# Both maps' attention scores in one PSUM tile of two banks, and PSUM pools opened anew for each stage

## Chip, core and metric

The kernel runs on one core of a Trainium2 chip. The metric is device time in microseconds (us), the median of several runs. The engines are TensorE (PE; PEld is its weight load), VectorE (DVE), ScalarE (ACT), GpSimd (POOL) and SyncE (SP), which issues the loads.

## What is computed

One layer of an encoder over 512 positions of width 1024: a normed and modulated input is projected, three mixers (differential attention, two gated recurrences) run on it, their results are projected up, gated and summed, and an MLP follows. The part that the change touches is the differential attention, with 4 heads, two maps of 64 dimensions in each, and blocks of 128 queries:

```python
scores = jnp.einsum('bhiqd,bhikd->bhiqk', qb, k).astype(jnp.float32) * scale
scores = scores - slopes[:, None, None, None] * dist
p = jax.nn.softmax(scores, axis=-1)
w = p[:, :, 0] - lam * p[:, :, 1]
return jnp.einsum('bhqk,bhkv->bhqv', w.astype(v.dtype), v)
```

Index i is the map: two softmaxes over the same 512 keys, of which the second is subtracted with a weight.

## The kernel before

All large products are made of fp32r matmuls in three parts: a weight and an input are each split into a high and a low part, and `mm3` (lines 219 to 222) issues high by high, high by low and low by high into one PSUM bank. One such matmul streams 512 columns through all 128 rows of the array.

**PSUM.** It has 8 banks of 128x512 fp32. Pool `pm` has 3 for projections (`ps_mm`), `pl` has 3 (`ps_lv`) and `pt` 2 (`ps_ms`). `pl` serves the scans' level scores first and the attention's scores later; `pt` serves transposes, the attention's output and the norms' statistics. The pools are open from the first stages to the kernel's end.

**Attention** (`attention(hd)`, lines 784 to 818). For each of 4 heads and each of 4 blocks of queries, two tiles of `pl` are taken, one for each map. Each map has three matmuls (q high by k high, q high by k low, q low by k high), 6 in all, 96 in the kernel. A map has 64 dimensions, so map 0 uses rows 0 to 63 of the array and map 1 rows 64 to 127 (line 795). Then DVE adds the distance penalty and takes the row maximum (line 800, one operation for each map, which is the only reader of the score's bank), ACT takes the exponential (line 803), DVE normalises and subtracts the maps (lines 806 to 809), PE transposes the result in four pieces (line 812, tile `wt`) and ACT copies these out (line 814). After the four blocks of a head PE multiplies with the values (line 817, tile `oa`), and `head_norm` (lines 630 to 639) norms the head: a square on ACT, a matmul with a matrix of constants for the mean (line 634, tile `An..ms`), a logarithm and an exponential on ACT, a product on DVE, and a split into a high part (ACT, `An..oh`) and a low part (DVE, `An..ol`).

**Work around it.** `merge_bc(m)` for m = 0 to 7 projects the gates `gb`, `gc` (24 matmuls each) and the two recurrences' results `up` (6 matmuls each), combines them on DVE (lines 834 and 836, tiles `gbs`, `gcs`, `part`), and then takes four tiles of the modulation's weights, `ada`: each is loaded (512 KB) and reduced by one DVE operation (line 164). `att_proj` projects q and k of heads 2 and 3, `proj_a` the gates `ga`. `pump(NA)` in `attention` starts pieces of this work between the steps of a block. Behind the attention, a loop over m (lines 860 to 874) multiplies the four normed heads with `wup_a` into a bank of `pm` (`upa`), after `ga` of the same m.

**Order.** In this stage the order on each engine is not the order of the code: the framework's scheduler places each instruction where its own timeline lets it start, and each engine then runs its list in that order. A tile's pool hands out its buffers in turn, and the first writer of a buffer waits for the last reader of what it held. Raw weights and `ada` tiles share one ring of four SBUF buffers (tag `wr` of pool `wp`), and all their loads stand in SyncE's queue in order, each waiting for its buffer to come free. `weights` (lines 209 to 217) loads a raw tile, and ACT and DVE make its high part (line 215) and its low part (line 216).

Of the kernel before, what the change touches and what calls it, by code (L numbers as in the profile page):

```python
# [11 lines left out]
F32 = mybir.dt.float32  # L12
# [5 lines left out]
PSUM = bass.MemoryType.PSUM  # L18

P = 128  # L20
S = 512
# [33 lines left out]
def tile_trunk(ctx, tc, xT, cols, lam_p, w2blk, ada, slab, wtok, wlr, wck, wcq, wg, watt, wgate, wup_bc, wup_a, wout,  # L55
# [4 lines left out]
    def pool_of(name, n, side="left"):  # L60
        return tc.tile_pool(name=name, bufs=n, side=side, reuse_waits="tile")
# [15 lines left out]
    sm = ms_.enter_context(pool_of("sm", 4))  # L77
    sm.tile([P, 8], F32, tag="fill", name="smfill")
    pm = ctx.enter_context(tc.tile_pool(name="pm", bufs=3, space=PSUM))
    pl = ctx.enter_context(tc.tile_pool(name="pl", bufs=3, space=PSUM))  # L80

    def st(name, dt=F32, pool=None):
        return (pool or gp).tile([P, S], dt, tag="t", name=name)
# [4 lines left out]
    def ps_lv(name):  # L88
        return pl.tile([P, S], F32, tag="lv", name=name)

    def ps_ms(name):
        return pt.tile([P, S], F32, tag="ms", name=name)
# [102 lines left out]
    def pump(n):  # L195

        while queue and n > 0:
            try:
                next(queue[0])
                n -= 1  # L200
            except StopIteration:
                queue.popleft()
# [67 lines left out]
    with tc.tile_pool(name="ad0", bufs=8, side="right", reuse_waits="tile") as ad0, \  # L270
# [54 lines left out]
        for k in range(KT):  # L325
# [12 lines left out]
            f = t  # L338
# [13 lines left out]
                for u in us:  # L352
                    mm3(slab_ps[u], wh[:, u * P:(u + 1) * P], wl[:, u * P:(u + 1) * P], hi, lo, False, k == KT - 1)
        lb, neglam, gsub, gb40, masks, bm, w2b, nd = small_operands()
    pt = ctx.enter_context(tc.tile_pool(name="pt", bufs=2, space=PSUM))

    def proj(src, name):
        wh, wl = weights(src, name, [P, KT, P])
# [271 lines left out]
    def head_norm(o, n, blk, g, extra, pool, dst):  # L630
        sq = st(n + "sq", pool=pool)
        A.activation(sq, o, AF.Square)
        ms = ps_ms(n + "ms")
        T.matmul(ms, blk, sq, start=True, stop=True)
        rs = rstd_of(ms, n + "rs", pool)
        V.scalar_tensor_tensor(sq, o, g, rs, ALU.mult, ALU.mult)  # L636
        if extra is not None:
            V.scalar_tensor_tensor(sq, sq, 0.5, extra, ALU.mult, ALU.mult)
        return split(sq, n + "o", dst)
# [133 lines left out]
    zs.close()  # L773
    ys.close()
    zs, ys = ExitStack(), ExitStack()
    oap = zs.enter_context(pool_of("oap", 8))
    fp = ys.enter_context(pool_of("fp", 8, "right"))
    es = ExitStack()
# [5 lines left out]
    def attention(hd):  # L784
        slope = 2.0 ** (-2 * (hd + 1))
        qh, ql, kh, kl = qk[hd]
        wT = [st(f"wT{hd}{k}", pool=wtp) for k in range(4)]
        for qt in range(4):
            qs = slice(qt * P, (qt + 1) * P)
            e = []  # L790
            mx = sm.tile([P, 8], F32, tag="mx", name=f"mx{hd}{qt}")
            sc = [ps_lv(f"s{hd}{qt}{i}") for i in range(2)]
            for n_, (q_, k_) in enumerate(((qh, kh), (qh, kl), (ql, kh))):
                for i in range(2):
                    rr = slice(64 * i, 64 * i + 64)
                    T.matmul(sc[i], q_[rr, qs], k_[rr, :], start=n_ == 0, stop=n_ == 2)  # L796
            pump(NA)
            for i in range(2):
                s_ = st(f"e{hd}{qt}{i}", pool=ep)
                V.tensor_tensor_reduce(s_, sc[i], nd[:, 384 - P * qt:896 - P * qt], scale=slope, scalar=-3e38,  # L800
                                       op0=ALU.add, op1=ALU.max, accum_out=mx[:, i:i + 1])
                V.tensor_scalar(mx[:, 2 + i:3 + i], mx[:, i:i + 1], -1.0, None, ALU.mult)  # L802
                A.activation(s_, s_, AF.Exp, bias=mx[:, 2 + i:3 + i], accum_out=mx[:, 4 + i:5 + i])  # L803
                e.append(s_)
            pump(NA)
            V.reciprocal(mx[:, 6:8], mx[:, 4:6])
            V.tensor_tensor(mx[:, 7:8], mx[:, 7:8], neglam, ALU.mult)
            V.tensor_scalar(e[0], e[0], mx[:, 6:7], None, ALU.mult)  # L808
            V.scalar_tensor_tensor(e[0], e[1], mx[:, 7:8], e[0], ALU.mult, ALU.add)  # L809
            ps = ps_ms(f"wt{hd}{qt}")  # L810
            for k in range(4):
                T.transpose(ps[:, k * P:(k + 1) * P], e[0][:, k * P:(k + 1) * P], ident)  # L812
            for k in range(4):
                A.copy(wT[k][:, qs], ps[:, k * P:(k + 1) * P])  # L814
        o = ps_ms(f"oa{hd}")
        for k in range(4):
            T.matmul(o, av[k][:, hd * P:(hd + 1) * P], wT[k], start=k == 0, stop=k == 3)  # L817
        oa.append(head_norm(o, f"An{hd}", ones128, gsub, None, ep, oap))
# [35 lines left out]
    for hd in range(4):  # L854
        need(f_att[hd])
        attention(hd)
# [19 lines left out]
    zs.close()  # L876
    ys.close()
    ms_.close()

    gtm = lambda m: modc[:, 16 + m:17 + m]  # L880
    amlp = const.tile([P, 8], F32, name="amlp")
# [304 lines left out]
    with tc.manual_schedule(engines=ENGINES):  # L1186
# [227 lines left out]
        for u in range(4, 16):  # L1414
            g, i = divmod(u, 4)
# [161 lines left out]
```

## Time and profile before

| | us |
|---|---|
| median of 3 runs (lowest, highest) | 866.3 (865.47, 867.59) |
| time of the profiled execution | 868.18 |
| its span | 866.3 |
| PE busy | 848.4 (98%) |
| PE's weight loads busy | 718.4 (83%) |
| DVE busy | 602.9 (70%) |
| ACT busy | 431.3 (50%) |
| chain of work that ended last, on PE | 94% |

The span runs from the first to the last instruction of the execution. An engine's busy time counts its operations alone; matmuls are pipelined, so that the distance between two starts, not the length of one, is what a matmul costs. A timeline gives the start, the length, the engine, the line of the code and the tiles; a number in brackets is idle time before the instruction, with what ended it. `x2` stands for two instructions shown in one row.

### The profile page before, as it was taken

Reading aid. Unit: us, or ns where it says so; the run is one execution under the profiler, and the core shown is the slowest. Engines: PE = TensorE matmul, PEld = TensorE weight load, DVE = VectorE, ACT = ScalarE, POOL = GpSimd, SP = SyncE. Lnnn points to the kernel's source line nnn. Section 1 sums busy time; section 2 is a strip of 40 time slices with the busy share of each in tenths; the row PEclk is TensorE's granted clock in tenths of the full one; section 3 lists DMA queues with packets and bytes.
Section 4 is the critical chain, followed back from the end, with each engine's and each line's share of the span. In section 5 each row is a group of like instructions: output and inputs, shape, how many; then the busy total and the mean of one; then the engine's idle time right before and its main releaser. Section 6 shows DMA issues by size and latency. Waiting matters only on the chain.

```text
span 866.3 us, 14040 instructions
## 1 busy us (share of the span) xinstructions
PE 848.4 (98%) x5632; PEld 718.4 (83%) x5632; DVE 602.9 (70%) x1077; ACT 431.3 (50%) x783; POOL 25.1 (3%) x33
## 2 busy tenths in 40 slices
PE   6999999999999999999999999999999999999995
PEld 3797888888777776777788899999999999999885
DVE  7968899595677685866166658766666666766445
ACT  5577887554354454446344436833444443444323
POOL 3700000000000000000000000000000000000000
PEclk9999999999999999999999999999999999999998
DMA  9933111112636454553134501332323323333202
GB/s 342 400 109 121 51 50 51 50 42 70 207 110 206 135 162 144 206 193 122 61 98 145 175 21 55 115 100 98 98 98 98 98 98 104 113 104 119 76 23 98
DMA packets 32817, 103.15 MB, mean 119 GB/s; under 512 B 3665, under 2 KB 6129, under 8 KB 32753
## 3 DMA queue, kind: packets, MB, share of 16 engines
q1 hardware_dynamic: 32752, 102.26, 35.9%
q8 instruction: 44, 0.72, 0.3%
q14 instruction: 21, 0.16, 0.1%
HBM read 100.15 MB, written 2.10 MB: 118 GB/s over the span
## 4 chain that ended last, share of the span: by engine, by line
PE 94%; DVE 3%; ACT 1%; DMA 1%; issue 0%; SPq 0%; DVEq 0%; ACTq 0%
PE w L222 7%; PE w L221 7%; PE w L220 7%; PE s L796 2%; PE ou L221 2%; PE ou L222 2%; PE ou L220 2%; PE tp L375 2%; PE oa L817 2%; PE tp L376 2%; PE tp L377 2%; PE sl L221 1%; PE sl L222 1%; PE sl L220 1%; PE up L220 1%; PE wt L812 1%
## 5 line engine op out<-in xcount | busy, mean ns | idle before, releaser
L164 DVE CUSTOM_DVE_ANT_0 ada<-ada,cb,col 128x1024 f32<-128x1024 f32 x32 | 41.1, 1283 | 32.9 <-DMA ada<-ada 32.9
L1157 DVE SCALAR_TENSOR_TENSOR x<-w,modc,x 128x512 f32<-128x512 f32 (+1 forms) x35 | 24.6, 703 | 32.6 <-PE w L222 32.6
L803 ACT ACTIVATE e<-e,mx 128x512 f32<-128x512 f32 x32 | 22.9, 719 | 23.9 <-DVE mx L802 23.9
L800 DVE CUSTOM_DVE_ANT_0 e<-s,nd 128x512 f32<-128x512 f32 x32 | 20.8, 685 | 0.0
L164 DVE CUSTOM_DVE_ANT_0 ada<-ada,cps,col 128x1024 f32<-128x1024 f32 x16 | 19.9, 1271 | 0.9 <-ACT cb L295 0.9
L814 ACT COPY wT<-wt 128x128 f32<-128x128 f32 x64 | 12.2, 279 | 13.4 <-PE wt L812 13.3
L1120 DVE SCALAR_TENSOR_TENSOR r<-r 128x512 f32<-128x512 f32 x24 | 16.5, 688 | 0.4
L817 PE MATMUL oa<-wT,av 128*128 128x512 f32 x32 | 14.4, 592 | 0.0
L915 DVE SCALAR_TENSOR_TENSOR x<-ou,modc,x 128x256 f32<-128x256 f32 (+1 forms) x12 | 6.8, 570 | 10.6 <-PE ou L222 10.6
L809 DVE SCALAR_TENSOR_TENSOR e<-e,mx,e 128x512 f32<-128x512 f32 x16 | 12.0, 750 | 0.3
L869 DVE SCALAR_TENSOR_TENSOR gas<-gas,upa 128x512 f32<-128x512 f32 x8 | 5.4, 686 | 9.0 <-PE upa L222 9.0
L336 ACT ACTIVATE hf<-hf,modc,amix 128x512 f32<-128x512 f32 x7 | 5.7, 817 | 12.0 <-DVE modc L164 8.3
L926 ACT ACTIVATE q<-x 128x256 f32<-128x256 f32 (+1 forms) x11 | 5.2, 470 | 13.0 <-DVE x L915 13.0
L1166 ACT ACTIVATE q<-x 128x256 f32<-128x256 f32 (+1 forms) x9 | 4.6, 514 | 13.4 <-DVE x L1157 13.4
L817 PEld LDWEIGHTS oa<-wT,av 128*128 128x128 f32 x32 | 6.0, 189 | 6.1 <-issue 5.5
L812 PEld LDWEIGHTS wt<-ident,e 128*128 128x128 f32 x64 | 7.6, 140 | 3.0 <-issue 0.7
L812 PE MATMUL wt<-ident,e 128*128 128x128 f32 x64 | 9.8, 275 | 0.0
L309 POOL TENSOR_TENSOR hf<-x,rx 128x512 f32<-128x512 f32 x7 | 9.5, 1357 | 0.0
L872 ACT ACTIVATE mgh<-part 128x512 fp32r<-128x512 f32 x8 | 5.0, 632 | 7.2 <-DVE part L870 7.2
L636 DVE SCALAR_TENSOR_TENSOR Hn1sq<-H1o,col,Hn1rsl 128x512 f32<-128x512 f32 x1 | 0.8, 750 | 10.9 <-ACT Hn1rsl L178 10.9
L636 DVE SCALAR_TENSOR_TENSOR An3sq<-oa,gsub,An3rsl 128x512 f32<-128x512 f32 x1 | 0.8, 751 | 10.8 <-ACT An3rsl L178 10.8
L808 DVE TENSOR_SCALAR e<-e,mx 128x512 f32<-128x512 f32 x16 | 7.7, 481 | 0.0
(7148 smaller groups left out, 3318.2 us busy)
## 6 DMA issues: line engine op xcount, KB each, us to landing
ada<-ada SPq DMA_DIRECT2D x48, 512.0 KB, 4.4
x<-xT SPq DMA_DIRECT2D x16, 256.0 KB, 4.4
outT<-o SPq DMA_DIRECT2D x8, 256.0 KB, 2.2
w10r<-w SPq DMA_DIRECT2D x2, 512.0 KB, 6.5
w11r<-w SPq DMA_DIRECT2D x2, 512.0 KB, 5.2
w12r<-w SPq DMA_DIRECT2D x2, 512.0 KB, 3.7
w13r<-w SPq DMA_DIRECT2D x2, 512.0 KB, 3.6
w14r<-w SPq DMA_DIRECT2D x2, 512.0 KB, 3.2
```

Of the source, the lines that this page charges most:

```text
L164: V.tensor_tensor_reduce(w, w, c_, scale=1.0, scalar=C("ada_b", ADA_BLK[u]), op0=ALU.mult, op1=ALU.add, accum_out=o)
L220: T.matmul(ps, wh, xh, start=first, stop=False)
L221: T.matmul(ps, wh, xl, start=False, stop=False)
L222: T.matmul(ps, wl, xh, start=False, stop=last)
L375: T.matmul(o, hh, wh, start=k == 0, stop=False)
L376: T.matmul(o, hh, wl, start=False, stop=False)
L377: T.matmul(o, hl, wh, start=False, stop=k == KT - 1)
L800: V.tensor_tensor_reduce(s_, sc[i], nd[:, 384 - P * qt:896 - P * qt], scale=slope, scalar=-3e38, op0=ALU.add, op1=ALU.max, accum_out=mx[:, ...
L803: A.activation(s_, s_, AF.Exp, bias=mx[:, 2 + i:3 + i], accum_out=mx[:, 4 + i:5 + i])
L812: T.transpose(ps[:, k * P:(k + 1) * P], e[0][:, k * P:(k + 1) * P], ident)
L817: T.matmul(o, av[k][:, hd * P:(hd + 1) * P], wT[k], start=k == 0, stop=k == 3)
L1157: V.scalar_tensor_tensor(x, self.ps[:, sl], modc[:, 40 + self.m:41 + self.m], x, ALU.mult, ALU.add)
```

## The change

The PSUM pools `pl` and `pt` move to an own stack, `banks`, which is closed and opened again ahead of the attention and behind it. For the attention there is a pool `pd` with one buffer of two banks, which holds the scores of both maps of one block, and `pt` has three banks where it had two; `pm` keeps its three. Behind the attention `pl` and `pt` have three and two banks again.

```diff
-    pl = ctx.enter_context(tc.tile_pool(name="pl", bufs=3, space=PSUM))
+    banks = ctx.enter_context(ExitStack())
+    pl = banks.enter_context(tc.tile_pool(name="pl", bufs=3, space=PSUM))
...
-    pt = ctx.enter_context(tc.tile_pool(name="pt", bufs=2, space=PSUM))
+    pt = banks.enter_context(tc.tile_pool(name="pt", bufs=2, space=PSUM))
...
     zs, ys = ExitStack(), ExitStack()
+    banks.close()
+    pd = banks.enter_context(tc.tile_pool(name="pd", bufs=1, space=PSUM))
+    pt = banks.enter_context(tc.tile_pool(name="pt2", bufs=3, space=PSUM))
...
-            sc = [ps_lv(f"s{hd}{qt}{i}") for i in range(2)]
+            both = pd.tile([P, 2, S], F32, tag="s", name=f"s{hd}{qt}")
+            sc = [both[:, i, :] for i in range(2)]
...
     ms_.close()
+    banks.close()
+    pl = banks.enter_context(tc.tile_pool(name="pl2", bufs=3, space=PSUM))
+    pt = banks.enter_context(tc.tile_pool(name="pt3", bufs=2, space=PSUM))
```

No operation is added or taken away. Line numbers of the changed kernel are higher by 7 at the scores (796 becomes 803) and by 1 in `mm3` (220 to 222 become 221 to 223). The scheduler orders the stage anew. Three places show it. The digits behind `s`, `e` and `mx` are head and block, then the map; a number behind an underscore is the buffer's.

**PE, scores of head 0.** Before, the three matmuls of map 1 of block 1 (`s011`) stand alone, those of map 0 some rows earlier; block 2 follows six rows later:

```order
L222 MATMUL up02_2836<-Gn1oh_2685,ubc0l_2721 128x512
L796 MATMUL s011_2801<-k0h_2383,qh0_2284 128x512
L796 MATMUL s011_2801<-k0l_2384,qh0_2284 128x512
L796 MATMUL s011_2801<-k0h_2383,ql0_2285 128x512
L220 MATMUL up10_2864<-Hn0oh_1402,ubc1h_2860 128x512
L221 MATMUL up10_2864<-Hn0ol_1403,ubc1h_2860 128x512
L222 MATMUL up10_2864<-Hn0oh_1402,ubc1l_2861 128x512
L220 MATMUL up10_2864<-Hn1oh_1740,ubc1h_2860 128x512
L221 MATMUL up10_2864<-Hn1ol_1741,ubc1h_2860 128x512
L222 MATMUL up10_2864<-Hn1oh_1740,ubc1l_2861 128x512
L796 MATMUL s020_2893<-k0h_2383,qh0_2284 128x512
L796 MATMUL s021_2894<-k0h_2383,qh0_2284 128x512
```

In the changed kernel (`x2` is one matmul of each map) the six of block 1 stand together:

```order
L223 MATMUL up12_2878<-Gn1oh_2685,ubc1l_2867 128x512
L803 MATMUL s01_2807<-k0h_2383,qh0_2284 128x512 x2
L803 MATMUL s01_2807<-k0l_2384,qh0_2284 128x512 x2
L803 MATMUL s01_2807<-k0h_2383,ql0_2285 128x512 x2
L221 MATMUL aq2p_2927<-h0h_254,aq2h_2923 128x512
L222 MATMUL aq2p_2927<-h0l_255,aq2h_2923 128x512
```

What moved: all 16 blocks now have their six score matmuls in one piece, where the order before had 18 pieces: 13 with three matmuls of one map or six of two, one of three that four transposes cut in two, and four of nine matmuls, in which the second map of one block is followed by the next block (or a whole block by the first map of the next).

**DVE, head 2, block 0.** Before, the two operations that read the scores (`e200`, `e201`) stand behind three `ada` tiles:

```order
L164 ISA ada37_3767,modc_158<-ada37_3767,cb_157,col_129 128x1024
L164 ISA modc_158 128x1
L216 TENSOR_TENSOR gb5l_3625<-gb5r_3622,gb5h_3624 128x1024
L164 ISA ada38_3770,modc_158<-ada38_3770,cb_157,col_129 128x1024
L164 ISA modc_158 128x1
L882 SCALAR_TENSOR_TENSOR amlp_4638<-modc_158,col_129 128x8
L800 ISA e200_3507,mx20_3469<-s200_3470,nd_555 128x512
L800 ISA mx20_3469 128x1
L800 ISA e201_3511,mx20_3469<-s201_3471,nd_555 128x512
L800 ISA mx20_3469 128x1
L800 ISA e210_3591,mx21_3555<-s210_3556,nd_555 128x512
```

In the changed kernel they stand behind four of the next group of `ada` tiles, which follow `gcs4`, `ubc5l` and `part4` directly:

```order
L165 ISA ada40_3941,modc_158<-ada40_3941,cb_157,col_129 128x1024
L165 ISA modc_158 128x1
L165 ISA ada41_3944,modc_158<-ada41_3944,cb_157,col_129 128x1024
L165 ISA modc_158 128x1
L217 TENSOR_TENSOR gb6l_3775<-gb6r_3772,gb6h_3774 128x1024
L165 ISA ada42_3947,modc_158<-ada42_3947,cb_157,col_129 128x1024
L165 ISA modc_158 128x1
L165 ISA ada43_3950,modc_158<-ada43_3950,cb_157,col_129 128x1024
L165 ISA modc_158 128x1
L807 ISA e200_3506,mx20_3469<-s20_3470,nd_555 128x512
L807 ISA mx20_3469 128x1
L807 ISA e201_3510,mx20_3469<-s20_3470,nd_555 128x512
```

What moved: the readers of block 0 of head 2 went behind `ada40` to `ada43`. On PE the next block's scores (`s21`) then stand behind `gb5`, `gc5`, `up50` and `up52`, with `wt13`, `oa1` and the statistic of head 1 among them; before, `s211` stood behind `up42`.

**PE, end of the last head.** Before, 11 matmuls of `ga3` and nine of `upa1` (the last three are shown) stand between the statistic `An3ms` and the first matmul that reads the normed head (`An3oh`), and work of `ga4` follows:

```order
L220 MATMUL upa1_4327<-An2oh_3841,ua1h_4323 128x512
L221 MATMUL upa1_4327<-An2ol_3842,ua1h_4323 128x512
L222 MATMUL upa1_4327<-An2oh_3841,ua1l_4324 128x512
L220 MATMUL upa0_4269<-An3oh_4219,ua0h_4265 128x512
L220 MATMUL upa1_4327<-An3oh_4219,ua1h_4323 128x512
L220 MATMUL ga4p_4352<-h0h_254,ga4h_4348 128x512
L221 MATMUL ga4p_4352<-h0l_255,ga4h_4348 128x512
L222 MATMUL ga4p_4352<-h0h_254,ga4l_4349 128x512
L220 MATMUL ga4p_4352<-h1h_292,ga4h_4348 128x512
L221 MATMUL ga4p_4352<-h1l_293,ga4h_4348 128x512
```

In the changed kernel `An3ms` is followed by nine matmuls of `upa2` alone, and then by `An3oh`:

```order
L635 MATMUL An3ms_4205<-An3sq_4203,ones128_116 128x512
L221 MATMUL upa2_4377<-An0oh_3085,ua2h_4373 128x512
L222 MATMUL upa2_4377<-An0ol_3086,ua2h_4373 128x512
L223 MATMUL upa2_4377<-An0oh_3085,ua2l_4374 128x512
L221 MATMUL upa2_4377<-An1oh_3461,ua2h_4373 128x512
L222 MATMUL upa2_4377<-An1ol_3462,ua2h_4373 128x512
L223 MATMUL upa2_4377<-An1oh_3461,ua2l_4374 128x512
L221 MATMUL upa2_4377<-An2oh_3837,ua2h_4373 128x512
L222 MATMUL upa2_4377<-An2ol_3838,ua2h_4373 128x512
L223 MATMUL upa2_4377<-An2oh_3837,ua2l_4374 128x512
L221 MATMUL upa0_4261<-An3oh_4211,ua0h_4257 128x512
L221 MATMUL upa1_4319<-An3oh_4211,ua1h_4315 128x512
```

What moved: `ga3` and most of `ga4` are done earlier in the changed kernel, and all three banks of `pm` hold an `upa` when the last head's norm is under way. On ACT the changed order has the cast of `ua2h` and the gate `gas4` between the head's square and the table load; before, the table load followed the square directly.

## Rows read from the trace of the kernel before

**Rows 1.** Window: span, busy us (instructions) by engine, clock, DMA, GB/s.

```profile
200.00:300.00 100.00, 100.00 (x530) 75.77 (x530) 69.38 (x137) 46.50 (x89) 0.00 (x0) 1.00 0.49 150
```

**Rows 2.** Timeline of PE, six paired scores: start, us, engine, line, tile.

```profile
235.37 0.51 PE L796 MATMUL s<-k0h,qh 64*128 64x512 f32 x2
...
236.28 0.50 PE L220 MATMUL up<-Hn0oh,ubc0h 128*128 128x512 f32 x1
236.62 0.39 PE L221 MATMUL up<-Hn0ol,ubc0h 128*128 128x512 f32 x1
```

**Rows 3.** Timeline of PE, three score matmuls alone.

```profile
247.53 0.39 PE L220 MATMUL gc1p<-h5h,gc1h 128*128 128x512 f32 x1
247.76 0.39 PE L221 MATMUL gc1p<-h5l,gc1h 128*128 128x512 f32 x1
248.08 0.49 PE L796 MATMUL s<-k0h,qh 64*128 64x512 f32 x1
...
248.97 0.50 PE L222 MATMUL gc1p<-h5h,gc1l 128*128 128x512 f32 x1
```

**Rows 4.** Timeline of PE, nine score matmuls and the row before.

```profile
341.24 0.39 PE L222 MATMUL up<-Gn1oh,ubc4l 128*128 128x512 f32 x1
341.56 0.51 PE L796 MATMUL s<-k2h,qh 64*128 64x512 f32 x2
...
343.14 0.50 PE L220 MATMUL gb5p<-h0h,gb5h 128*128 128x512 f32 x1
```

**Rows 5.** Timeline of DVE: in brackets the idle time before, and what ended it.

```profile
327.81 1.28 DVE L164 CUSTOM_DVE_ANT_0 ada<-ada,cb,col 128x1024 f32<-128x1024 f32 x1 [4.42 <-DMA ada<-ada]
...
333.42 1.28 DVE L164 CUSTOM_DVE_ANT_0 ada<-ada,cb,col 128x1024 f32<-128x1024 f32 x1 [4.31 <-DMA ada<-ada]
...
338.37 1.29 DVE L164 CUSTOM_DVE_ANT_0 ada<-ada,cb,col 128x1024 f32<-128x1024 f32 x1 [2.52 <-DMA ada<-ada]
...
339.78 0.68 DVE L800 CUSTOM_DVE_ANT_0 e<-s,nd 128x512 f32<-128x512 f32 x1
```

**Rows 6.** Tile ada, 300 to 345 us: issue of a load to landing.

```profile
DMA to landing us min/median/max: 3.4/4.2/4.9
```

**Rows 7.** Timeline of DVE behind the projection up4.

```profile
345.47 0.68 DVE L834 SCALAR_TENSOR_TENSOR gcs<-gcs,up 128x512 f32<-128x512 f32 x1
...
349.16 0.69 DVE L216 TENSOR_TENSOR ubc5l<-ubc5r,ubc5h 128x512 fp32r<-128x512 f32 x1
```

**Rows 8.** Timeline of SyncE, the issue of a load of ada.

```profile
349.88 0.33 SPq L158 DMA_DIRECT2D ada<-ada  x1
```

**Rows 9.** Timeline of DVE, the first ada tile behind ubc2l.

```profile
271.10 0.68 DVE L216 TENSOR_TENSOR ubc2l<-ubc2r,ubc2h 128x512 fp32r<-128x512 f32 x1
...
275.73 1.28 DVE L164 CUSTOM_DVE_ANT_0 ada<-ada,cb,col 128x1024 f32<-128x1024 f32 x1 [1.09 <-DMA ada<-ada]
```

**Rows 10.** Timeline of PE at the end of the last head.

```profile
415.87 3.59 PE L817 MATMUL oa<-wT,av 128*128 128x512 f32 x8
418.90 0.79 PE L220 MATMUL upa<-An0oh,ua0h 128*128 128x512 f32 x1
...
424.31 1.02 PE L634 MATMUL An3ms<-An3sq,ones 128*128 128x512 f32 x2
```

**Rows 11.** Timeline of ACT at the same place.

```profile
419.50 0.60 ACT L632 ACTIVATE An3sq<-oa 128x512 f32<-128x512 f32 x1 [2.50 <-PE oa L817]
420.12 1.28 ACT L177 ACT_TABLE_LOAD   x1
425.37 0.69 ACT L177 ACTIVATE An3rsl<-An3ms,eps 128x512 f32<-128x512 f32 x1 [3.96 <-PE An3ms L634]
...
428.85 0.61 ACT L184 CAST An3oh<-An3sq 128x512 fp32r<-128x512 f32 x1
```

**Rows 12.** Timeline of PE near the start: the longest wait with work behind it.

```profile
22.98 0.50 PE L220 MATMUL sl<-h1h,wsl1h 128*128 128x512 f32 x1 [2.71 <-ACT h1h L337]
```

**Rows 13.** Windows near the start, columns as in Rows 1.

```profile
24.00:28.00 4.00, 4.00 (x12) 3.08 (x12) 3.96 (x7) 2.17 (x3) 3.53 (x3) 0.57 1.03 406
```

## Prediction

> **What bounds the kernel now.** First the windows: in the 100 us in which the attention begins PE is busy for all 100, with the full clock granted, DVE for 69 and ACT for 47 [rows 1]. So the stage ends with PE; what a change takes from PE's list, or adds to it as a wait, arrives in the total, and the other engines matter where PE waits for them. Then the timeline of PE, where the distance of two starts is the cost. An ordinary matmul of 512 columns costs 0.23 us (247.53 to 247.76) [rows 3]. Then the timeline of DVE around 330 us: it stands still for 4.42, 4.31 and 2.52 us ahead of three `ada` tiles, each time for the load, and reads the scores of head 2, block 0 only behind them, at 339.78 [rows 5]. PE does not wait for that in the kernel before, since three banks hold scores ahead. This is the fact on which the change turns: DVE runs late behind loads, and the number of score banks decides whether PE feels it.
>
> **What the change takes away.** Six score matmuls, alternately in the two halves of the array, cost 0.91 us (235.37 to 236.28) [rows 2]; three of one half alone cost 0.89 (248.08 to 248.97) [rows 3]. So the second map is free if it stands beside the first. Entering a piece stretches the matmul before it to 0.32 (247.76 to 248.08), 0.09 more than 0.23 [rows 3], and leaving it stretches the one behind to 0.34 (236.28 to 236.62), 0.11 more [rows 2]. A piece of three or six costs 0.90 + 0.20 = 1.1 us. One of nine costs 341.56 to 343.14, 1.58, and 0.20 of entry and exit: 1.78 [rows 4]. The order before has 14 pieces of the first sort (the one cut by transposes counted as plain, which is a little too low) and 4 of the second: 15.4 + 7.1 = 22.5 us. The changed order has 16 plain pieces, 17.6 us. **The gain is 4.9 us.** All of it lies on PE, which has no idle time there, so all of it counts.
>
> **What it adds: waits on PE.** With one score tile the first matmul of a block waits for both readers of the block before, on DVE. PE runs its list in order, so everything behind that matmul waits too: gates, projections, transposes and the attention's output. I go through the places where the changed order puts a reader behind loads.
>
> *Head 2, block 1 (`s21`).* In the changed order of DVE `gcs4`, `ubc5l`, `part4`, `ada40`, `ada41`, `gb6l`, `ada42`, `ada43` stand ahead of the two readers of block 0. The load of `ada40` is issued when `ubc5l` ends: in the trace 349.16 + 0.69 = 349.85, and the issue follows at 349.88 [rows 7, 8]. It lands 4.2 us later (3.4 to 4.9) [rows 6]. From one `ada` to the next, whose load waits for the buffer of the one before, it is 5.6 and 4.95 us [rows 5]; I count these two for `ada40` to `ada42`. `ada43` is loaded shortly behind `ada42` and follows at its length, 1.3. Then come its own 1.3 and the two readers, 2 x 0.68. Sum from the issue: 4.2 + 5.6 + 4.95 + 1.3 + 1.3 + 1.4 = 18.7. Ahead of the issue `gcs4` and `ubc5l` take 1.3. `gcs4` needs the end of `up42` on PE: 341.24 + 0.39 = 341.63 [rows 4]; it started at 345.47 [rows 7], 3.84 later, because DVE was late. At best this lateness is 0. So the readers end 20.0 to 23.8 us behind `up42`. PE in the same time has `wt13` (some 0.4), 60 matmuls (`gb5`, `gc5`, `up50`, `up52`) at 0.23 = 13.8, `oa1` at 3.03 (415.87 to 418.90) and a statistic at some 0.9 (its rows take 1.02, of which part overlaps) [rows 10]: 18.1. The wait is between 1.9 and 5.7 us. I take 5.4, near the end that the row with 3.84 gives, since in the changed order too DVE comes to `gcs4` straight from the `ada` tiles of the group before.
>
> A rule speaks for a smaller price. The Trainium skill, in TensorE: Matmul & The Clock Gate, section "HAM oscillation — how this bites in real kernels", reports of a matmul kernel that double-buffering in PSUM "gave no further gain". By that one buffer would do here, and the sum would be without the waits of the scores. The lateness of DVE [rows 5, 7] speaks against it here; the kernel of the page is not this one.
>
> *Head 1, block 0 (`s10`).* Its tile is free when DVE has read block 3 of head 0, which stands behind `ubc2l`, the end of two blocks' softmax and `ada28`. In the trace the `ada` behind `ubc2l` starts 275.73 - 271.79 = 3.9 us after it [rows 9]; with 1.3 for itself and 1.4 for the readers that is 6.6. PE comes to `s10` from the transposes `wt02`, which need a softmax that ends some 2 us behind `ubc2l`. So the wait is at most 4.6 and at least 0; DVE's and PE's lists between have nearly the same length, so I take 1.5.
>
> *End of the last head.* Let T be the end of `oa3`; in the trace 415.87 + 3.59 = 419.46, and PE issues the next matmul at 418.90, T - 0.56 [rows 10]. ACT squares from 419.50 for 0.60, loads a table for 1.28, starts the logarithm at 425.37 and has the high part at 428.85 + 0.61 = 429.46 [rows 11], 4.09 after the logarithm's start. In the changed order ACT does a cast and a gate (0.6 each) between the square and the table. The high part is there at T + 0.04 + 0.6 + 1.2 + 1.28 + 4.09 = T + 7.2; if the two extra operations hid elsewhere, at T + 6.0. PE has three matmuls of `ga4` (T + 0.1), waits 0.5 for the square, does the statistic (T + 1.5) and nine matmuls (2.1): it stands at T + 3.6. The wait is 0.5 + 2.4 to 3.6, and behind it `ga5` waits for weights that ACT split late and for a bank, 0 to 1.4. I take 4.4 (2.9 to 5.5). Before, 20 matmuls and the work of `ga4` covered this; the changed order has used them up, and `pm` has no free bank.
>
> *Other blocks.* One more reader or weight just late: 0 to 1.5, I take 0.5.
>
> *Clock.* Near the start PE waits 2.71 us [rows 12], and in the 4 us behind it the granted clock is 0.57, partly at 1.2 GHz in place of 2.4 [rows 13]: (1 - 0.57) x 4 = 1.7 us lost. A wait of over 5 us at `s21` should cost the same again; that at the end of the head may. I count 1.7 once (0 to 3.4).
>
> **Sum.** -4.9 + 5.4 + 1.5 + 4.4 + 0.5 + 1.7 = +8.6. The span of the profiled execution, 866.3, equals the median, so 866.3 + 8.6 = **875 us**. All low ends give -4.9 + 1.9 + 0 + 2.9 = -0.1 (866), all high ends -4.9 + 5.7 + 4.6 + 5.5 + 1.5 + 3.4 = +15.8 (882).
>
> **Rivals.**
> 1. *DVE keeps pace, the scores wait nowhere; only the last head's end costs.* -4.9 + 4.4 = -0.5: 866 us. For it: PE never waited in this stage before. Against it: 339.78 as the reading of scores that PE wrote long before [rows 5]. The skill's sentence on double-buffering would lead here.
> 2. *Faster: the last head's end is hidden too*, because ACT's chain is shorter than I count or PE comes later than the order says. -4.9: 861 us. It decides if PE stands behind T + 6 instead of T + 3.6; nothing in the order gives it the work.
> 3. *The pairs do not run beside each other in a tile of two banks.* Then a block costs six slots, 6 x 0.23 + 0.2 = 1.6, 16 of them 25.6, 3.1 more than before, and with the waits and the clock: 866.3 + 3.1 + 13.5 = 883 us. Against it: the halves of the array and the two banks alternate as in the paired pieces of before [rows 2].
>
> **How the numbers follow.** About 0.3%, 2.6 us, is what a measurement of this kernel can tell from no change: 863.7 to 868.9. Forecast 0.80, rival 1 (no change) 0.09, rival 2 (faster) 0.06, rival 3 (slower) 0.05. So faster 0.06, same 0.09, slower 0.85. The range of 8 in 10 leaves out rivals 2 and 3 and nearly all of 1, and of the forecast's own spread only that in which all prices meet one end: 868.5 to 881.
>
> **What would show it.** In the changed profile: 16 pieces of scores, each 0.9 us, with two matmuls in a row; if single ones stand there, the gain is wrong. PE idle ahead of the scores (line 803) by 5 us in one place and 1 to 2 us in another, released by DVE's line 807; if the idle is below 2 us in all, rival 1 holds. PE idle for 3 to 4 us ahead of `upa`, released by the last head's cast on ACT. A granted clock below 1 in the 4 us behind the longest wait. DVE's and ACT's busy times unchanged. The prediction fails above all if DVE reaches `gcs4` early, or if the loads of `ada` overlap where I count them in a row.

## The result, and the profile after

The changed kernel takes 876.8 us (median of 4 runs, 876.3 to 879.1), the kernel before, in the same session, 866.7. The ratio is 1.0118, 95% interval [1.0105, 1.0132]: 10.1 us slower. The forecast was 875.0, in a range of 868.5 to 881.

The profiled executions stand 10.9 us apart (span 877.2 against 866.3). The number of instructions on PE is the same, DVE's and ACT's busy times are too (603.6 and 432.1 us; before 602.9 and 431.3).

What the loss consists of is told by the waits of PE from 215 to 470 us: line waited at, what was waited for, us in total, times, longest. Before, this answer has no row.

```profile
PE s L803 <- DVE mx L807: 6.2, 2, 5.3
PE upa L221 <- ACT An3oh L185: 3.0, 1, 3.0
PE wt L819 <- DVE e L816: 1.5, 1, 1.5
PE ga5p L223 <- DVE ga5l L217: 0.3, 1, 0.3
```

The longest, in PE's timeline (start, us, engine, line, tile; idle time and its cause in brackets) with the rows behind it:

```profile
358.30 0.79 PE L803 MATMUL s<-k2h,qh 64*128 64x512 f32 x2 [5.33 <-DVE mx L807]
358.89 0.63 PE L803 MATMUL s<-k2l,qh 64*128 64x512 f32 x2
359.32 0.63 PE L803 MATMUL s<-k2h,ql 64*128 64x512 f32 x2
```

The last two starts are 0.43 us apart here; in an undisturbed piece they are 0.23 apart (below). The chain of the work that ended last, in the same stretch, names the cause step by step (start, us, what): three loads of `ada`, the first and the last issued behind a weight's split (`ubc5l`, `gb6l`), the second when the `ada` before has been read, and at their end the two readers on line 807 and the scores on PE.

```profile
338.33 0.61 DVE ubc5l L217
...
338.96 4.22 DMA ada<-ada
...
343.32 1.28 DVE ada L165
344.64 3.56 DMA ada<-ada
...
349.62 1.15 DVE gb6l L217
350.79 4.80 DMA ada<-ada
...
357.02 0.60 DVE e L807
...
358.30 1.65 PE s L803 x6
```

DVE's timeline there, which answers to [rows 5, 7], shows the same from its side: it stands still for 3.79, 3.72, 2.41 and 1.26 us ahead of the four `ada`, and the scores of head 2, block 0, which PE had written at 324, are read at 356.94.

```profile
337.65 0.68 DVE L841 SCALAR_TENSOR_TENSOR gcs<-gcs,up 128x512 f32<-128x512 f32 x1
...
343.32 1.28 DVE L165 CUSTOM_DVE_ANT_0 ada<-ada,cb,col 128x1024 f32<-128x1024 f32 x1 [3.79 <-DMA ada<-ada]
...
355.72 1.28 DVE L165 CUSTOM_DVE_ANT_0 ada<-ada,cb,col 128x1024 f32<-128x1024 f32 x1 [1.26 <-DMA ada<-ada]
...
356.94 0.69 DVE L807 CUSTOM_DVE_ANT_0 e<-s,nd 128x512 f32<-128x512 f32 x1
```

At the end of the last head, ACT's timeline (which answers to [rows 11]) and PE from the last statistic to the wait:

```profile
438.76 0.60 ACT L633 ACTIVATE An3sq<-oa 128x512 f32<-128x512 f32 x1 [7.11 <-PE oa L824]
...
439.76 0.60 ACT L400 ACTIVATE gas<-ga4p 128x512 f32<-128x512 f32 x1
...
441.67 0.69 ACT L178 ACTIVATE An3rsl<-An3ms,eps 128x512 f32<-128x512 f32 x1
...
445.12 0.62 ACT L185 CAST An3oh<-An3sq 128x512 fp32r<-128x512 f32 x1 [0.82 <-DVE An3sq L637]
```

```profile
439.41 1.13 PE L635 MATMUL An3ms<-An3sq,ones 128*128 128x512 f32 x2
440.41 0.51 PE L221 MATMUL upa<-An0oh,ua2h 128*128 128x512 f32 x1
...
445.79 0.50 PE L221 MATMUL upa<-An3oh,ua0h 128*128 128x512 f32 x1 [3.04 <-ACT An3oh L185]
```

The windows behind the two long waits (span, busy us and instructions of PE, PEld, DVE, ACT, POOL, granted clock, DMA share, GB/s): the clock is at half, 1.2 GHz in place of 2.4.

```profile
358.00:364.40 6.40, 6.10 (x17) 4.39 (x18) 6.40 (x17) 2.66 (x6) 0.00 (x0) 0.50 0.50 132
446.60:450.00 3.40, 3.40 (x10) 2.63 (x10) 2.18 (x4) 2.63 (x4) 0.00 (x0) 0.51 0.00 0
```

And an undisturbed piece of scores, two maps beside each other, 302.36 to 303.26 = 0.90 us; all 16 pieces have six matmuls:

```profile
302.36 0.50 PE L803 MATMUL s<-k1h,qh 64*128 64x512 f32 x2
302.70 0.40 PE L803 MATMUL s<-k1l,qh 64*128 64x512 f32 x2
302.93 0.39 PE L803 MATMUL s<-k1h,ql 64*128 64x512 f32 x2
303.26 0.50 PE L221 MATMUL aq3p<-h0h,aq3h 128*128 128x512 f32 x1
```

The account of the loss in these two executions: waits 0.89 + 5.33 (both `s`) + 1.48 (`wt`) + 3.04 + 0.33 = 11.1; half clock 6.1 x 0.50 + 3.4 x 0.49 = 4.7; the pieces of scores, by their lengths in the two traces and 0.20 each for entry and exit, 22.9 before and 17.6 after at the full clock, -5.3. Together +10.5.

The loss itself is larger than the 10.9 us between the spans, because this execution of the changed kernel came to the stage 1.3 us earlier. From the statistic `Gn0ms` ahead of the stage to the first `ou` behind it PE takes 235.4 us before (first fence) and 247.6 us after (second), 12.2 more:

```profile
234.05 1.02 PE L634 MATMUL Gn0ms<-Gn0sq,blk 128*128 128x512 f32 x2
...
469.42 0.39 PE L220 MATMUL ou<-mgh,wo0h 128*128 128x512 f32 x1
```

```profile
232.70 1.02 PE L635 MATMUL Gn0ms<-Gn0sq,blk 128*128 128x512 f32 x2
...
480.29 0.39 PE L221 MATMUL ou<-mgh,wo0h 128*128 128x512 f32 x1
```

So the account lacks 1.7 us. Some 0.8 of them lie in how idle time is counted: from the end of the matmul before, 0.39 us behind its start, although the next ordinary one would have started after 0.23; that is 0.16 too little in each of five waits. Another 0.5 is a wait that the list doesn't have: the matmul behind `An3ms` starts 1.00 us after it (439.41 to 440.41), where it was 0.46 before (424.31 to 424.77), since `upa2` takes the bank of `ga4`, which ACT reads until 440.36. The last 0.4 are not accounted for. The profiled execution was also the longest of the four (879.1), so the medians stand less far apart than these two executions.

### The profile page after: what moved, and what is told of

It is laid out like the page before. It is cut to its first block, busy times and chain, and to the rows that moved or that the text cites. A ratio compares the mean times of both kernels' runs of the same rounds, so it can differ in the third digit from the quotient of the medians.

```text
span 877.2 us, 14028 instructions
## 1 busy us (share of the span) xinstructions
PE 850.4 (97%) x5632; PEld 718.8 (82%) x5632; DVE 603.6 (69%) x1077; ACT 432.1 (49%) x783; POOL 25.2 (3%) x33
## 4 chain that ended last, share of the span: by engine, by line
PE 86%; DMA 5%; DVE 4%; ACT 2%; issue 1%; POOL 1%; SPq 0%; DVEq 0%
PE w L222 7%; PE w L223 7%; PE w L221 7%; DMA ada<-ada 4%; PE ou L222 2%; PE ou L221 2%; PE ou L223 2%; PE tp L376 2%; PE tp L377 2%; PE tp L378 1%; PE s L803 1%; PE oa L824 1%; PE sl L222 1%; PE sl L223 1%; PE sl L221 1%
## 5 line engine op out<-in xcount | busy, mean ns | idle before, releaser
L810 ACT ACTIVATE e<-e,mx 128x512 f32<-128x512 f32 x32 | 22.9, 716 | 16.5 <-DVE mx L809 16.4
L637 DVE SCALAR_TENSOR_TENSOR Hn1sq<-H1o,col,Hn1rsl 128x512 f32<-128x512 f32 x1 | 0.8, 750 | 10.9 <-ACT Hn1rsl L179 10.9
L803 PE MATMUL s<-k2h,qh 64*128 64x512 f32 x8 | 2.3, 571 | 5.3 <-DVE mx L807 5.3
```

## The experiments

Two theories stand against each other. **Mine**: the pairs save about 5 us, and the single tile takes more than that back because DVE reads the scores late, behind the loads of `ada`; the end of the last head costs a second wait, because the gates that covered it are used up. **The rivals**: reopening the pools costs; two banks are simply too few; the tile makes PE wait wherever its readers stand; the pairs save nothing. Times of before are those of the same chip. The 876.8 of the changed kernel is from an earlier session, in which before took 866.7; if each time is taken against before of its own session, the gains against the changed kernel that are named below are 0.2 to 0.4 us smaller.

### Reopening alone

```diff
-    pd = banks.enter_context(tc.tile_pool(name="pd", bufs=1, space=PSUM))
-    pt = banks.enter_context(tc.tile_pool(name="pt2", bufs=3, space=PSUM))
+    pd = banks.enter_context(tc.tile_pool(name="pd", bufs=3, space=PSUM))
+    pt = banks.enter_context(tc.tile_pool(name="pt2", bufs=2, space=PSUM))
...
-            both = pd.tile([P, 2, S], F32, tag="s", name=f"s{hd}{qt}")
-            sc = [both[:, i, :] for i in range(2)]
+            sc = [pd.tile([P, S], F32, tag="s", name=f"s{hd}{qt}{i}") for i in range(2)]
```

> The pools closed and opened again at both places, but with three banks in single tiles for the scores and two for the rest, as before. Theory (reopening costs nothing, since the banks are handed over one by one): 866.7, between 866 and 867.5, no PE wait in the stage. Rival (part of the loss comes from the reopening): up to 876.8.

Measured: 865.9 us, ratio 1.0005 [0.9989, 1.0021], no wait of PE in the stage. The reopening costs nothing that shows.

### The four `ada` tiles moved

```diff
         for u in range(16 + 4 * m, 20 + 4 * m):
-            ada_tile(u, ada_load(u), cb)
+            if m not in (6,):
+                ada_tile(u, ada_load(u), cb)
...
+    held = [40, 41, 42, 43]
     for m in range(KT):
...
         V.tensor_tensor(part[m], part[m], ga, ALU.add)
+        for u in held[4 * m:4 * m + 4]:
+            ada_tile(u, ada_load(u), cb)
```

> The changed kernel, but the four ada tiles 40 to 43 (load and DVE operation) are moved from the middle of the attention to behind the first gate product of the loop after it; on DVE the two readers of head 2, block 0 then follow part4 directly. Theory (PE waits for the scores' tile because DVE reaches the readers late, behind these loads): the wait of 5.33 us ahead of the scores of head 2, block 1 and the stretch at half clock behind it (358.3 to 364.4, 6.1 us, so 3.0 lost) go; 876.8 - 8.3 = 868.5, between 867 and 870; the wait of about 3 us at the end of the last head stays. Rival (one tile makes PE wait for its two readers wherever they stand): a wait of over 3 us stays there, over 874.

Measured: 869.6 us, ratio to before 1.0036 [1.0023, 1.0049], so 7.2 less than the changed kernel; 8.3 were expected. On DVE the readers follow the gate's split (345.58), 11.4 us earlier than in the changed kernel, and PE's waits have lost the long one:

```profile
PE upa L221 <- ACT An3oh L185: 3.0, 1, 3.0
PE s L803 <- DVE mx L807: 1.4, 1, 1.4
PE wt L819 <- DVE e L816: 1.0, 1, 1.0
...
```

No operation was taken away, nothing of the tile was changed: the wait came from where the readers stood behind four loads, and the rival that the tile alone makes it falls.

### The readers first

```diff
-                V.tensor_tensor_reduce(s_, sc[i], nd[:, 384 - P * qt:896 - P * qt], scale=slope, scalar=-3e38,
-                                       op0=ALU.add, op1=ALU.max, accum_out=mx[:, i:i + 1])
+                with tc.high_priority():
+                    V.tensor_tensor_reduce(s_, sc[i], nd[:, 384 - P * qt:896 - P * qt], scale=slope, scalar=-3e38,
+                                           op0=ALU.add, op1=ALU.max, accum_out=mx[:, i:i + 1])
```

> The changed kernel with high priority for the readers of the scores, which puts those of head 2, block 0 ahead of ada42 and ada43, behind ada40 and ada41. Theory: the wait of 5.33 us shrinks by about two loads' distance minus what is behind, to some 1 to 2.5 us, the clock does not fall there or half as long; the readers that come earlier put gates and weights later, and some waits under 1 us appear; 876.8 - 3 to -5, 873, between 870 and 876. Rival (readers' place on DVE is not what PE waits for): 876.8.

Measured: 873.1 us, ratio 1.0078 [1.0062, 1.0094]. In head 2 PE now waits 0.80 where it waited 5.33, and 1.35 ahead of a later block's scores, and 1.54 ahead of the first block of head 3:

```profile
348.47 0.50 PE L803 MATMUL s<-k2h,qh 64*128 64x512 f32 x2 [0.80 <-DVE mx L810]
366.21 0.50 PE L803 MATMUL s<-k2h,qh 64*128 64x512 f32 x2 [1.35 <-DVE mx L810]
373.60 0.49 PE L803 MATMUL s<-k3h,qh 64*128 64x512 f32 x2 [1.54 <-DVE mx L808]
```

Priority alone shortens the longest wait and gives part of it back in others: DVE is still behind the loads, only with other work. The wait at the end of the last head stays (3.06).

### The end of the last head

```diff
-LA = 2
+LA = 3
...
-        ps = ps_mm(f"upa{m}")
+        ps = ps_ms(f"upa{m}")
```

> The changed kernel with two edits at the end of the last head alone: one more gate projection allowed ahead (LA 3), and the products of the normed heads in the pool of three banks that the transposes had, so that the gates keep the banks of pm; 27 matmuls of upa0 to upa2 then stand between the last statistic and its first use, where nine stood. Theory: of the 3.4 us of waits and 1.7 us of half clock there, short waits of under 1 us each remain, some 1 to 3 us in all; 876.8 - 3 = 873.8, between 872 and 875.5; the wait of 5.33 us at head 2 stays. Rival (the tail is bound by ACT's chain whatever stands ahead of it): 876.8.

Measured: 873.3 us, ratio 1.0078 [1.006, 1.0095], 3.5 less than the changed kernel. Between the last statistic (441.70) and the first product with the normed head PE has its 27 matmuls, and the wait of 3.04 is gone; around this place waits of 0.51, 0.41, 0.22 and 0.59 remain, and from 440 to 460 the clock is 1.00. The wait at head 2 stays, at 5.67. So the two losses are separate, and the second is worth 3.5 us with its half clock; the forecast had 4.4 (2.9 to 5.5) without it.

### Two single banks in place of the double one

```diff
-    pd = banks.enter_context(tc.tile_pool(name="pd", bufs=1, space=PSUM))
+    pd = banks.enter_context(tc.tile_pool(name="pd", bufs=2, space=PSUM))
...
-            both = pd.tile([P, 2, S], F32, tag="s", name=f"s{hd}{qt}")
-            sc = [both[:, i, :] for i in range(2)]
+            sc = [pd.tile([P, S], F32, tag="s", name=f"s{hd}{qt}{i}") for i in range(2)]
```

> The changed kernel with two tiles of one bank for the scores in place of one of two banks, so with the same two banks. Theory (the waits come from the tile, which is free only when both readers are done, and from the order that it brings; the pairs come from it too): no PE wait in the stage, but 26 pieces of scores, of which 20 with three matmuls of one map and four with five slots; by 1.1 us a piece and 1.57 for those of five slots 30.5 us, 8 more than before: 874, between 872 and 875.5. Rival (two banks are too few, tile or not): waits of over 5 us as in the changed kernel, and the missing pairs on top, 882 or more.

Measured: 871.2 us, ratio 1.006 [1.0045, 1.0075], no wait of PE in the stage. With the same two banks the waits are gone, and with them the pairs: 20 of the 26 pieces hold three matmuls of one map, as this one, 253.21 to 254.10 = 0.89 us, which is what six cost in a pair:

```profile
253.21 0.50 PE L802 MATMUL s<-k0h,qh 64*128 64x512 f32 x1
...
254.10 0.50 PE L221 MATMUL aq2p<-h0h,aq2h 128*128 128x512 f32 x1
```

26 pieces, by their lengths in the trace and 0.20 each, take 28.4 us, 5.5 more than before; the time is 4.9 more. I had expected 8 and no time below 872, mostly because I counted four pieces at five slots; they took 0.9 like the rest, which the next run explains. Two banks are not too few, and that rival falls.

### The six matmuls map by map

```diff
-            for n_, (q_, k_) in enumerate(((qh, kh), (qh, kl), (ql, kh))):
-                for i in range(2):
+            for i in range(2):
+                for n_, (q_, k_) in enumerate(((qh, kh), (qh, kl), (ql, kh))):
```

> The changed kernel with the six score matmuls of a block in another order: the three of map 0, then the three of map 1, so that only the fourth can start beside the third. Theory (pairs run beside each other in the tile of two banks, three slots for six matmuls): a block takes five slots, 2 x 0.235 us more, 16 x 0.47 = 7.5 us more on PE; since PE comes later to the waits and DVE doesn't, the waits of 0.9, 1.5 and 5.3 us shrink by 3 to 4: 880.5, between 878 and 884. Rival (the tile of two banks already keeps the pairs apart): no change, 877, and the pieces of scores are as long as in the changed kernel.

Measured: 877.1 us, ratio 1.0125 [1.0107, 1.0143]: no change against the changed kernel, and my expectation missed. Not because the pairs stand apart, as the rival had it, but because they run beside each other in this order too:

```profile
302.88 0.50 PE L803 MATMUL s<-k1h,qh 64*128 64x512 f32 x2
303.21 0.40 PE L803 MATMUL s<-k1l,qh 64*128 64x512 f32 x2
303.45 0.40 PE L803 MATMUL s<-k1h,ql 64*128 64x512 f32 x2
303.77 0.50 PE L221 MATMUL aq3p<-h0h,aq3h 128*128 128x512 f32 x1
```

In PE's list the three of map 0 now stand ahead of the three of map 1, yet each product still starts in both maps at nearly the same time (`x2`), and the piece takes 0.89 us. The step that failed is the five slots: I took it that PE starts matmuls in the order of its list. Since it leaves the pairs as they are, this run doesn't measure what they are worth. Its waits fell differently (1.25, 3.10 and 3.06, and one of 1.68 behind the first scores of head 2), 9.4 us in all. The 1.68 is not for scores: the gate `gc4p` takes the bank of `aq3p`, whose reader on DVE (`ql`, line 747) stands behind an `ada` tile here (325.83 to 326.51) and stood ahead of it in the changed kernel (323.35).

### A second buffer for the pairs

```diff
-    pm = ctx.enter_context(tc.tile_pool(name="pm", bufs=3, space=PSUM))
     banks = ctx.enter_context(ExitStack())
+    pm = banks.enter_context(tc.tile_pool(name="pm", bufs=3, space=PSUM))
...
-    pd = banks.enter_context(tc.tile_pool(name="pd", bufs=1, space=PSUM))
-    pt = banks.enter_context(tc.tile_pool(name="pt2", bufs=3, space=PSUM))
+    pm = banks.enter_context(tc.tile_pool(name="pm2", bufs=2, space=PSUM))
+    pd = banks.enter_context(tc.tile_pool(name="pd", bufs=2, space=PSUM))
+    pt = banks.enter_context(tc.tile_pool(name="pt2", bufs=2, space=PSUM))
...
+    pm = banks.enter_context(tc.tile_pool(name="pm3", bufs=3, space=PSUM))
     pl = banks.enter_context(tc.tile_pool(name="pl2", bufs=3, space=PSUM))
```

> The changed kernel with two buffers of two banks for the scores; the four banks are paid by the projections (pm has two banks in place of three during the attention) and the transposes (two in place of three). Theory (one bank fewer for the projections makes PE wait for the gates' readers on DVE and ACT, which are as late as the scores' readers): the wait of 5.33 us goes, but several waits of 0.5 to 4 us stand elsewhere, in all some 6 to 10 us; 872, between 868 and 876. Rival (a second buffer is all that was missing): no wait in the stage, 862.

Measured: 871.6 us, ratio 1.0052 [1.0037, 1.0067]. The wait of 5.33 is gone, and PE waits elsewhere, for scores and for the banks of gates:

```profile
PE s L804 <- DVE mx L808: 4.0, 3, 2.7
PE gb5p L221 <- DVE gbs L842: 1.3, 1, 1.3
PE upa L221 <- ACT gas L400: 0.7, 1, 0.7
...
```

A second buffer shortens the waits, but it isn't all that was missing: with two buffers PE still waits some 4 us for scores. The waits for the banks of gates are not its doing alone, since this run also took a bank from the projections; a second buffer beside three banks for the projections was not run.

### The third bank of `pt` unused

```diff
-    pt = banks.enter_context(tc.tile_pool(name="pt2", bufs=3, space=PSUM))
+    pt = banks.enter_context(tc.tile_pool(name="pt2", bufs=2, space=PSUM))
```

> The changed kernel with two banks for transposes and the attention's output in place of three, so that one bank is never used. Theory (the third bank has no part in the loss and none in a gain): 876.8, between 875.5 and 878, with the same two longest waits. Rival (the third bank covers transposes that would wait otherwise): 878 or more.

Measured: 878.8 us, ratio 1.014 [1.0123, 1.0157], 0.8 above what I had expected and inside the rival's range. But the instructions stand in the same order on every engine, the span of the profiled execution is the same (877.2), and so are the two longest waits (5.69 and 3.06). The intervals of the two kernels overlap; whether the third bank is worth a microsecond or two stays open.

### The pairs without the waits

Three edits against the waits (`ada` 40 to 47 moved as above, the readers first, one more gate projection allowed ahead), put on the changed kernel and, for comparison, on the single banks of before (three for scores, two for `pt`):

```diff
-LA = 2
+LA = 3
...
+                with tc.high_priority():
+                    V.tensor_tensor_reduce(s_, sc[i], nd[:, 384 - P * qt:896 - P * qt], scale=slope, scalar=-3e38,
...
-            ada_tile(u, ada_load(u), cb)
+            if m not in (6, 7):
+                ada_tile(u, ada_load(u), cb)
...
+    held = [40, 41, 42, 43, 44, 45, 46, 47]
...
+        for u in held[4 * m:4 * m + 4]:
+            ada_tile(u, ada_load(u), cb)
```

> The changed kernel with three edits: ada tiles 40 to 47 behind the gate products, the readers of the scores with high priority, and one more gate projection allowed ahead (LA 3 in place of 2), by which 24 matmuls of ga5 stand between the last head's statistic and its first use. Theory (the pairs save about 5 us on PE, and the waits ate them): no PE wait over 1 us in the stage, the full clock, 16 pieces of scores; 866.7 - 5.0 = 861.7, between 860 and 864. Rival (the stage ends with something else than PE, or the pairs save nothing): 866 or more.

> The same three edits with the scores in single banks out of three, as before. Theory (the edits only remove waits, and the kernel before had none): 866.7, between 865.5 and 868. Rival (the edits shorten the stage by themselves): as far below 866.7 as the paired kernel with these edits.

Measured: with pairs 860.8 us (10 runs), ratio 0.9947 [0.9932, 0.9962]; with single banks 866.2 us (10 runs), ratio 0.9999 [0.9988, 1.001]. The edits alone do nothing where nothing waited; the pairs are worth 866.2 - 860.8 = 5.4 us once nothing waits for them. The two kernels differ in the third bank of `pt` as well; the lengths of the pieces, which don't depend on it, gave 5.3. The window of the stage in the kernel with pairs:

```profile
230.00:430.00 200.00, 199.94 (x899) 149.53 (x900) 134.34 (x288) 99.51 (x215) 0.00 (x0) 1.00 0.47 154
```

On DVE the readers stand directly behind `part`, and PE writes the next block's scores some nine microseconds later without a wait. DVE's timeline, and PE's:

```profile
336.57 0.69 DVE L808 CUSTOM_DVE_ANT_0 e<-s,nd 128x512 f32<-128x512 f32 x1
```

```profile
347.07 0.50 PE L803 MATMUL s<-k2h,qh 64*128 64x512 f32 x2
```

At the end of the last head 24 matmuls of `ga5` stand between the statistic and the first product of the normed head, where the changed kernel had nine of `upa2`; the first and the last row:

```profile
427.60 1.02 PE L635 MATMUL An3ms<-An3sq,ones 128*128 128x512 f32 x2
...
433.94 0.39 PE L221 MATMUL upa<-An3oh,ua0h 128*128 128x512 f32 x1
```

This kernel beats both: 5.6 us below before, 16.0 below the change as it was made.

## Why the prediction was right, point by point

| step | forecast, us | measured, us | by |
|---|---|---|---|
| pairs | -4.9 | -5.4 | with and without pairs, no waits; the pieces' lengths |
| wait at `s21` | +5.4 (1.9 to 5.7) | +5.33 | trace; 7.2 with its clock when its loads were moved |
| wait at `s10` | +1.5 (0 to 4.6) | +0.89 | trace |
| end of the last head | +4.4 (2.9 to 5.5) | +3.04 + 0.33 | trace; 3.5 with its clock when covered |
| others | +0.5 (0 to 1.5) | +1.48 | trace |
| clock | +1.7 (0 to 3.4) | +4.7 | windows |
| sum of these terms | +8.6 | +10.4 | |

**Pairs.** Right in size, and the rival that they would not run beside each other in a tile of two banks falls with the piece of 0.90.

**The wait at `s21`.** The chain ran as forecast: the load issued as `ubc5l` ends (338.25 + 0.69 = 338.94, issue at 338.96), 4.2 us to its landing, then 5.0, 4.8 and 2.6 us from one `ada` to the next where I had counted 5.6, 4.95 and 1.3. `gcs4` was even later than in the row I had taken: `up42` ended at 332.84 and `gcs4` started at 337.65, 4.8 us instead of 3.84. The readers ended some 25.4 us behind `up42` (forecast 20.0 to 23.8), and PE came to `s21` 20.1 us behind `up42`, of which 1.48 were a wait at `wt13` (forecast 18.1, without a wait): both terms came out some 2 us longer. That their difference is so near the forecast is in part luck: without the wait at `wt13`, which I had not seen, it would have been about 6.8. The choice that decided it was to take DVE's lateness from the row and not from its best case. That this lateness is the cause, the run with the four tiles moved shows.

**`s10` and the end of the head.** The places were right, the sizes a little high. With T the end of `oa3`, 435.13 + 3.59 = 438.72, the high part is there at 445.12 + 0.62 = 445.74, T + 7.0 (forecast T + 7.2), and PE stands from 442.75 on, T + 4.0 (forecast T + 3.6). Ahead of the statistic PE lost 0.2 and not the 0.5 that I had for the square, since the three matmuls of `ga4` covered most of it; the 0.5 behind the statistic, for the bank of `upa2`, I had not seen. `ga5` waited 0.33.

**Others.** The wait of 1.48 at `wt` is for the softmax of head 1, block 3; I had looked at scores and weights only. DVE ended this softmax late because it stood 2.04 and 0.50 us for the loads of two `ada` tiles around it, so it is the same lateness at another place. It is gone in the relieved kernel.

**Clock.** This is the term that was mis-sized: I counted the fall once, at the price of the start of the kernel, and had the second as a bound. Both long waits were followed by half clock, for 6.1 and 3.4 us, 4.7 lost in all where I had 1.7. These 3.0 us more than explain the 1.8 by which the sum of the terms was short; the larger gain and the smaller waits at `s10` and at the end of the head took part of them back.

**Rivals.** Rival 1 (the scores wait nowhere) led to 866 and falls with the first row of the waits, and rival 2 (the end of the last head is hidden) with the 3.04. The sentence that stood beside rival 1, of the Trainium skill, TensorE: Matmul & The Clock Gate, section "HAM oscillation — how this bites in real kernels", that PSUM double-buffering "gave no further gain", is neither borne out nor refuted as it stands: the second buffer gained 876.8 - 871.6 = 5.2 us where DVE was late, although other pools paid for it with a bank each, and none was needed where DVE came in time (860.8 with one buffer). Whether one buffer is enough was a question of the readers.

## What to carry to other kernels

A buffer count is a promise about how late the readers may be: before taking one away, look for the reader's longest distance behind its writer in the timeline, and for what stands ahead of it (here 512 KB loads through a shared ring). A saving on the bounding engine is only worth its size if no wait comes with it; so make the readers early first, then take the buffer. And work that runs earlier than before is missing as cover where it stood.

## What the runs showed of the hardware that was not expected

The order of matmuls in the two halves of the array doesn't matter within a piece: three of map 0 followed by three of map 1 took 0.89 us, as alternating ones do, and with starts side by side. Where a matmul on all 128 rows stood between the maps, each three took 0.89, as in the kernel with two single banks. The kernel before could have told it: its list has, for the piece of [rows 4], three of `s211`, three of `s220` and three of `s221`, and the piece took 1.58 us, as one with six alternating ones did (306.99 to 308.58, 1.59).

The clock's fall doesn't follow from the length of a wait alone. In the changed kernel, behind the wait of 3.04 us, it stood at 0.51 for 3.4 us; behind one of 3.02 at the same place in the kernel with the `ada` tiles moved, it stayed at 1.00:

```profile
436.91 0.51 PE L221 MATMUL upa<-An3oh,ua0h 128*128 128x512 f32 x1 [3.02 <-ACT An3oh L185]
```

```profile
436.00:440.00 4.00, 3.09 (x12) 2.03 (x13) 2.49 (x5) 2.45 (x4) 0.00 (x0) 1.00 0.00 0
```

In the kernel with the readers first it was 0.64 behind a wait of 1.54 that followed two others:

```profile
373.00:377.00 4.00, 3.40 (x11) 2.30 (x12) 3.88 (x9) 1.95 (x6) 0.00 (x0) 0.64 1.00 378
```

In the kernel with the matmuls map by map it fell behind the wait of 1.68, the first in 50 us, while in the changed kernel it stayed at 1.00 (334 to 338) behind the 1.48 at `wt13`:

```profile
326.00:330.00 4.00, 3.43 (x8) 2.74 (x9) 2.92 (x6) 1.52 (x4) 0.00 (x0) 0.59 0.53 159
```

These are single executions. What decides was not tried; in a sum the half clock behind a wait is to be kept as a range, here from nothing to 3 us for one wait.
